# Two transformer blocks on one core: where the array's tiles begin, and value products with 128 columns

## The chip, the core and the metric

The kernel runs on one core of one Trainium2 chip. The core has a matrix engine (TensorE, PE in the profile; its weight loads are listed as PEld), a vector engine (VectorE, DVE), a scalar engine (ScalarE, ACT), GpSimd (POOL) and SyncE (SP), which issues most of the transfers. The metric is the device time of one execution in microseconds, the median over several runs.

## The reference

Two transformer blocks run one after the other on 512 tokens of width 1024, all in float32. The heart of it:

```python
# block 1
h = modulate(rmsnorm(x), ...);  proj = h @ w_in
s = q @ k.T * scale (+ rel_bias);  p = softmax(mask(s));  o = p @ v     # 8 MLA heads, 8 chunk-attention heads
x = x + g_a * (concat(o_mla, o_ca) @ w_out)
u = causal_dwconv(modulate(rmsnorm(x), ...) @ w_up);  x = x + g_m * ((silu(gate) * val) @ w_down)
# block 2
y_a = stick_breaking(q_a, k_a, v_a)          # 8 heads of 64: exp(log_sigmoid(z) + tail) @ v
y_b = retention(q_b, k_b, v_b)               # 8 heads of 64: (q k^T * decay) v, then group norm and gate
x = x + concat(y_a, y_b) @ w_out
x = x + moe(rmsnorm(x))                      # 32 experts, top 4, 1024 -> 2 x 1024 -> 1024
x = x + (p @ w_ple_proj) * sigmoid(rmsnorm(x) @ w_ple_gate)
```

A head is 64 wide in all three attentions' value products.

## The kernel before, in words

The stages follow one another: modulation and input projections to about 165 us, softmax attention to 285, output projection, the MLP's up projection from 400 to 570 and its down projection from 570 to 690, the projections of block 2, retention from 791 to 835, stick-breaking attention from 916 to 970, the experts from about 1060 to 2280, and the last gate.

**Dense products.** To keep float32 accuracy each large operand is split into a high and a low part in the array's one-pass format: `split` (L183) copies the value with ACT (L185) and subtracts with DVE (L188). A product is then three TensorE instructions (`mm3`): high by high, high by low, low by high. All of them go through `mm` (L165), so that the profile knows products by their tiles: `whi`/`wlo` and `hh`/`hl` are the parts of weights and of activations in block 1, `ah`/`al` the parts of the hidden activations, `mhi`/`mlo` the parts of the experts' weights `mraw`, `xh`/`xl` and `ah`/`al` the parts of an expert's 128 tokens. In the profile's rows the first name after the arrow is the moving operand, of 512 columns here, and the second the stationary one, of 128 columns. An f32 operand that is not split runs as one instruction that leaves two records.

**Attention.** The softmax attention goes through units (head, row block of 128 queries). At step s TensorE makes the scores of unit s, the transposes of unit s - 3 and the value product of unit s - 9. A value product (`pv`) has the head's 64 value columns as stationary operand and the transposed probabilities as moving one, with 512, 384, 256 or 128 columns. The two heads of a pair write the two halves, 64 partitions each, of one PSUM bank, and when the second head is done the bank is split into `hh` and `hl` at once. Retention (`rw` by `rv`) and stick-breaking (`sw` by `vs`) have the same layout, with 32 value products each; in the stick-breaking attention, whose products grow backwards over a bank, a product of a zero row first clears the pair's bank. PSUM has 8 banks of 128 x 512 that are handed out by `ps()`.

**Experts.** Weights come in chunks of 1 MB, issued by SP ahead of their use as buffers come free; ACT and DVE split each chunk; TensorE multiplies the split weights, as moving operand, by the tokens. The order on each engine is that of the program's text.

Of the kernel before, what the change touches and what calls it, by code (L numbers as in the profile page):

```python
# [10 lines left out]
F32 = mybir.dt.float32  # L11
F32R = mybir.dt.float32r
I32 = mybir.dt.int32
U32 = mybir.dt.uint32
AF = mybir.ActivationFunctionType
OP = mybir.AluOpType
# [6 lines left out]
NT = 4  # L23
P = 128
# [3 lines left out]
NE = 32  # L28
# [106 lines left out]
class Kernel:  # L135
# [343 lines left out]
    def softmax_attention(self, heads, pool, pool3, tail):  # L479
# [36 lines left out]
        def pv(hd, kt):  # L516
            par = hd["par"]
            if par == 0 and kt == 0:
                self.po = self.ps()
            rows = slice(64 * par, 64 * par + 64)  # L520
            self.mm(self.po[rows, kt * P:512], hd["v"](kt), hd["pT"][:, kt, kt * P:512], kt == 0, kt == NT - 1)
            if par == 1 and kt == NT - 1:
                return lambda po=self.po: self.split(po, self.hh[:, hd["pair"], :], self.hl_[:, hd["pair"], :])

# [40 lines left out]
    def block1(self, cg):  # L565
        nc, A = self.nc, self.A
        gp = self.pool("gp", 1, ctx=cg)
        self.ga = gp.tile([P, D], F32, name="ga")
        self.mcol = gp.tile([P, 48], F32, name="mcol")
        self.csil = gp.tile([P, 8], F32, name="csil")  # L570
# [167 lines left out]
        mp = self.pool("mla", 1, ctx=cm)  # L738
        gq = ap1.tile([P, 1], F32, name="gqs")
        nc.vector.tensor_scalar(gq, self.v("g_mq"), 96.0 ** -0.5, None, op0=OP.mult)  # L740
# [165 lines left out]
        for h in range(8):  # L906
            heads.append(dict(q=qTm[:, h, :], k=kTm[:, h, :], bias=None, par=h % 2, pair=h // 2,
                              v=lambda kt, h=h: vt[:, kt, h * 64:(h + 1) * 64]))
        for h in range(8):
            heads.append(dict(q=qTc[:, h // 2, :], k=kTc[:, h, :], bias=bias_for(h), par=h % 2,  # L910
                              pair=4 + h // 2, v=lambda kt, h=h: vc[:, kt, h * 64:(h + 1) * 64]))
        pso = []
# [122 lines left out]
    def block2_mix(self, right):  # L1035
        nc, A = self.nc, self.A
        cx = ExitStack()
        op = self.pool("o2", 1, ctx=cx)
        rx = op.tile([P, NT], F32, name="rx")
        self.row_rstd(self.ssx2, rx)  # L1040
# [38 lines left out]
        with ExitStack() as cr:  # L1079
# [48 lines left out]
            for s in range(len(units) + la):  # L1128
# [11 lines left out]
                if j >= 0:  # L1140
                    h, kt = units[j]
                    n = 512 - kt * P
                    rows = slice(64 * (h % 2), 64 * (h % 2) + 64)
                    if h % 2 == 0 and kt == 0:
                        po = self.ps()
                    self.mm(po[rows, kt * P:512], v[:, kt, h * 64:(h + 1) * 64], wt.pop(j)[:, 0:n], kt == 0,
                            kt == NT - 1)
                    if h % 2 and kt == NT - 1:
                        later = lambda h=h, po=po: nc.scalar.activation(yT[:, h // 2, :], po, AF.Copy)
            later()  # L1150
# [26 lines left out]
        self.zeros(qTs)  # L1177
        sc = os_.tile([P, 5, P], F32R, name="sc")
        idr, negr, trin, none, zero = [sc[:, i, :] for i in range(5)]
        for i, n in enumerate(("ident", "negm", "trin")):  # L1180
            nc.vector.tensor_copy(sc[:, i, :], self.cc(n))
        nc.vector.tensor_scalar(none, self.ones, -1.0, None, op0=OP.mult)
        nc.vector.tensor_scalar(zero, self.ones, 0.0, None, op0=OP.mult)
        cs = ExitStack()
# [35 lines left out]
        with ExitStack() as cs:  # L1220
# [7 lines left out]
            for s in range(len(units) + la3):  # L1228
# [35 lines left out]
                if 0 <= j < len(units):  # L1264
                    h, kt = units[j]
                    n = 512 - kt * P
                    rows = slice(64 * (h % 2), 64 * (h % 2) + 64)
                    if h % 2 == 0 and kt == 3:
                        po = self.ps()
                        self.mm(po, zero[0:1, :], sc[0:1, 0:4, :].rearrange("p a b -> p (a b)"), True, False)  # L1270
                    self.mm(po[rows, kt * P:512], vs[:, kt, h * 64:(h + 1) * 64], st.pop(j)[:, 0:n], False, kt == 0)
                    if h % 2 and kt == 0:
                        later[s + 2] = lambda h=h, po=po: self.split(po, self.hh[:, h // 2, :], self.hl_[:, h // 2, :])
        cx.close()
# [461 lines left out]
    def moe_open1(self, cx):  # L1736
# [6 lines left out]
        self.E4 = m1.tile([P, 2, NE], F32R, name="E4")  # L1743
        self.cnt = m1.tile([NE, 1], F32, name="cnt")
        for i in range(2):
# [24 lines left out]
    def moe_open3(self, cx):  # L1770
        self.mo = self.pool("mo", 1, ctx=cx, side="right")
        self.mo3 = self.pool("mo3", 6, ctx=cx, side="right")
        self.mx = self.pool("mx", 1, ctx=cx, side="right")
        m2 = self.pool("m2", 1, ctx=cx, side="right")
        self.xg = [m2.tile([P, D], F32, name="xg0")]
        self.g_n = 0
        self.nc.gpsimd.memset(self.xg[0], 0.0)
        self.ex = [self.expert(e) for e in range(NE)]
# [206 lines left out]
def build(nc, tc, A, out, dump=None):  # L1985
    with ExitStack() as ctx:
# [6 lines left out]
        K.ext = K.const.tile([1, 64], I32, name="ext")  # L1993
        K.extb = K.const.tile([P, 16], F32, name="extb")
        dr = K.pool("dr", 1, DRAM)
# [6 lines left out]
        with ExitStack() as right:  # L2002
            with ExitStack() as cr:
                big = K.pool("big", 1, ctx=cr)
                K.x = big.tile([P, NT, D], F32, name="x")
                K.ssx2 = big.tile([P, NT, 2], F32, name="ssx2")
                K.ssx3 = big.tile([P, NT, 2], F32, name="ssx3")
# [40 lines left out]
```

## Time and profile before

| what | value |
|---|---|
| median of 3 runs | 2365.99 us (2365.18 to 2371.5) |
| profiled execution | 2367.83 us |
| its span in the trace | 2365.7 us |
| TensorE busy | 2333.8 us, 99% of the span |
| VectorE busy | 1799.1 us, 76% |
| ScalarE busy | 1498.1 us, 63% |
| DMA traffic | 538.53 MB, mean 228 GB/s |

The profile is of one execution. Its own time is 1.8 us above the median, and its span is 2.1 us shorter than that time. A busy TensorE need not be at its peak: the time between the starts of two neighbouring products tells how fast it goes.

### The profile page before, as it was taken

The numbers are of one execution on the slowest core, as the hardware profiler recorded it, in microseconds if no ns is written. First come the engines' busy times: TensorE is split into PE (matmuls) and PEld (weight loads), VectorE is DVE, ScalarE is ACT, GpSimd is POOL, SyncE is SP. The second block draws the span as 40 slices with busy tenths as digits, with TensorE's granted clock in tenths as the row PEclk, the third lists the DMA queues.
The fourth block names the chain that finished last, engine by engine and source line by source line (L and its number), as shares of the span: only waits on it lengthen the run. The fifth ranks groups of instructions, "written<-read, shape, count | busy, mean of one in ns | idle before, by whom it ended". The sixth has DMA issues, their size and how long they took to land. (4 is left out here: it accounts for less than half of the span.)

```text
span 2365.7 us, 30628 instructions
## 1 busy us (share of the span) xinstructions
PE 2333.8 (99%) x10796; PEld 1849.6 (78%) x10796; DVE 1799.1 (76%) x2579; ACT 1498.1 (63%) x2201; POOL 165.1 (7%) x108
## 2 busy tenths in 40 slices
PE   9999999999999999989999999999999999999999
PEld 8874588888888576678888888888888888888877
DVE  6876676566557367559999999987799999999974
ACT  3676443334444237647778778775777778788764
POOL 0100000000000000010001101110010101101010
PEclk8999999999999999999999999999999999999999
DMA  9240333333233122259999999986999999999962
GB/s 326 88 131 13 123 115 125 115 108 108 98 109 99 43 89 72 96 185 337 334 356 342 356 351 342 361 295 218 330 361 356 347 358 335 362 346 342 332 198 107
DMA packets 282924, 538.53 MB, mean 228 GB/s; under 512 B 16277, under 2 KB 41397, under 8 KB 282576
## 3 DMA queue, kind: packets, MB, share of 16 engines
q1 hardware_dynamic: 268432, 508.08, 61.4%
q0 software_dynamic: 11792, 26.12, 4.1%
q10 hardware_dynamic: 2544, 2.34, 0.3%
q8 instruction: 86, 1.41, 0.2%
q14 instruction: 70, 0.57, 0.1%
HBM read 530.47 MB, written 23.59 MB: 234 GB/s over the span
## 5 line engine op out<-in xcount | busy, mean ns | idle before, releaser
L188 DVE TENSOR_TENSOR mlo<-mraw,mhi 128x1024 fp32r<-128x1024 f32 x777 | 911.3, 1219 | 118.7 <-ACT mhi L185 116.0
L185 ACT ACTIVATE mhi<-mraw 128x1024 fp32r<-128x1024 f32 x777 | 786.3, 1052 | 131.4 <-PE ps L165 110.4
L165 PE MATMUL ps<-mhi,xh 128*128 128x512 f32 x1024 | 409.6, 400 | 0.0
L165 PE MATMUL ps<-mhi,xl 128*128 128x512 f32 x1024 | 404.0, 395 | 0.2 <-DVE xl L1591 0.2
L165 PE MATMUL ps<-mlo,xh 128*128 128x512 f32 x1024 | 403.9, 394 | 0.0
L188 DVE TENSOR_TENSOR wlo<-raw,whi 128x1024 fp32r<-128x1024 f32 (+2 forms) x128 | 152.5, 1202 | 111.9 <-ACT whi L185 111.6
L165 PEld LDWEIGHTS ps<-mhi,xl 128*128 128x128 f32 x1024 | 192.7, 188 | 45.9 <-DVE xl L1591 0.6
L165 PEld LDWEIGHTS ps<-mlo,xh 128*128 128x128 f32 x1024 | 193.0, 188 | 42.4
L165 PEld LDWEIGHTS ps<-mhi,xh 128*128 128x128 f32 x1024 | 193.0, 188 | 41.3 <-ACT xh L1590 0.3
L185 ACT ACTIVATE whi<-raw 128x1024 fp32r<-128x1024 f32 (+2 forms) x128 | 132.5, 1042 | 135.0 <-PE ps L165 131.4
L165 PE MATMUL ps<-mhi,ah 128*128 128x512 f32 x512 | 203.1, 397 | 0.0
L165 PE MATMUL ps<-mhi,al 128*128 128x512 f32 x512 | 200.9, 392 | 0.0
L165 PE MATMUL ps<-mlo,ah 128*128 128x512 f32 x512 | 200.5, 392 | 0.0
L165 PE MATMUL ps<-whi,hh 128*128 128x512 f32 (+1 forms) x464 | 184.0, 397 | 5.1 <-ACT hh L185 2.3
L165 PE MATMUL ps<-wlo,hh 128*128 128x512 f32 (+1 forms) x464 | 180.8, 390 | 2.0 <-DVE wlo L188 2.0
L165 PE MATMUL ps<-whi,hl 128*128 128x512 f32 (+1 forms) x464 | 180.5, 389 | 0.0
L165 PE MATMUL ps<-hh,whi 128*128 128x512 f32 x352 | 137.8, 392 | 0.0
L165 PE MATMUL ps<-hh,wlo 128*128 128x512 f32 x352 | 136.9, 389 | 0.0
L165 PE MATMUL ps<-hl,whi 128*128 128x512 f32 x352 | 136.9, 389 | 0.0
L1644 ACT ACTIVATE mg<-mg 128x512 f32<-128x512 f32 x66 | 41.7, 632 | 141.5 <-DVE mg L1643 141.5
L165 PEld LDWEIGHTS ps<-mhi,al 128*128 128x128 f32 x512 | 96.1, 188 | 21.3
L165 PEld LDWEIGHTS ps<-mlo,ah 128*128 128x128 f32 x512 | 96.3, 188 | 20.4
(488 smaller groups left out, 3721.9 us busy)
## 6 DMA issues: line engine op xcount, KB each, us to landing
mraw<-in_w_ug SPq DMA_DIRECT2D x256, 1024.0 KB, 7.1
mraw<-in_w_dn SPq DMA_DIRECT2D x128, 1024.0 KB, 7.7
raw<-in_w_up SPq DMA_DIRECT2D x44, 512.0 KB, 3.6
raw<-in_w_in SPq DMA_DIRECT2D x40, 512.0 KB, 3.8
wa<-in_w_ada SPq DMA_DIRECT2D x12, 1024.0 KB, 11.8
raw<-in_w_ada SPq DMA_DIRECT2D x24, 512.0 KB, 4.6
raw<-in_w_down SPq DMA_DIRECT2D x22, 512.0 KB, 3.6
raw<-in_w_out SPq DMA_DIRECT2D x16, 512.0 KB, 4.8
```

The lines of the kernel that those rows point to most:

```text
L165: self.nc.tensor.matmul(out, l, r, start=start, stop=stop, skip_group_check=True)
L185: self.nc.scalar.activation(hi, raw, AF.Copy)
L188: self.nc.vector.tensor_tensor(lo, raw, hi, op=OP.subtract)
L1644: nc.scalar.activation(g, g, AF.Silu, scale=1.702)
```

## The change

It has three parts.

1. *Value products.* In all three attentions a head's value product takes the 128 value columns of its pair as stationary operand, writes all 128 partitions of a bank of its own, and only the head's 64 partitions of it are evacuated. The other 64 hold the neighbour's values under this head's probabilities and are not read. In place of one evacuation for each pair there is one for each head: 16 splits instead of 8 in the softmax attention, 8 copies instead of 4 in the retention, 8 splits instead of 4 in the stick-breaking attention.
2. *Zero products.* The stick-breaking attention's 4 zero products and their tile are gone; the first value product of a head starts its bank.
3. *Padding.* Some small tiles get more columns, which are not used, and one pool of small tiles 8 buffers instead of 6. What this does is to move the tiles that are allocated behind them.

```diff
-            par = hd["par"]
-            if par == 0 and kt == 0:
+            if kt == 0:
                 self.po = self.ps()
-            rows = slice(64 * par, 64 * par + 64)
-            self.mm(self.po[rows, kt * P:512], hd["v"](kt), hd["pT"][:, kt, kt * P:512], kt == 0, kt == NT - 1)
-            if par == 1 and kt == NT - 1:
-                return lambda po=self.po: self.split(po, self.hh[:, hd["pair"], :], self.hl_[:, hd["pair"], :])
+            self.mm(self.po[:, kt * P:512], hd["v"](kt), hd["pT"][:, kt, kt * P:512], kt == 0, kt == NT - 1)
+            if kt == NT - 1:
+                r = slice(64 * hd["par"], 64 * hd["par"] + 64)
+                return lambda po=self.po: self.split(po[r], self.hh[r, hd["pair"], :], self.hl_[r, hd["pair"], :])
...
-        self.mcol = gp.tile([P, 48], F32, name="mcol")
+        self.mcol = gp.tile([P, 96], F32, name="mcol")[:, 0:48]
...
-        gq = ap1.tile([P, 1], F32, name="gqs")
+        gq = ap1.tile([P, 56], F32, name="gqs")[:, 0:1]
...
-                              v=lambda kt, h=h: vt[:, kt, h * 64:(h + 1) * 64]))
+                              v=lambda kt, h=h: vt[:, kt, (h // 2) * P:(h // 2 + 1) * P]))
...
-        rx = op.tile([P, NT], F32, name="rx")
+        rx = op.tile([P, 56], F32, name="rx")[:, 0:NT]
...
-                    rows = slice(64 * (h % 2), 64 * (h % 2) + 64)
-                    if h % 2 == 0 and kt == 0:
+                    r = slice(64 * (h % 2), 64 * (h % 2) + 64)
+                    if kt == 0:
                         po = self.ps()
-                    self.mm(po[rows, kt * P:512], v[:, kt, h * 64:(h + 1) * 64], wt.pop(j)[:, 0:n], kt == 0,
+                    self.mm(po[:, kt * P:512], v[:, kt, (h // 2) * P:(h // 2 + 1) * P], wt.pop(j)[:, 0:n], kt == 0,
                             kt == NT - 1)
-                    if h % 2 and kt == NT - 1:
-                        later = lambda h=h, po=po: nc.scalar.activation(yT[:, h // 2, :], po, AF.Copy)
+                    if kt == NT - 1:
+                        later = lambda h=h, po=po, r=r: nc.scalar.activation(yT[r, h // 2, :], po[r], AF.Copy)
...
-                    if h % 2 == 0 and kt == 3:
+                    if kt == 3:
                         po = self.ps()
-                        self.mm(po, zero[0:1, :], sc[0:1, 0:4, :].rearrange("p a b -> p (a b)"), True, False)
-                    self.mm(po[rows, kt * P:512], vs[:, kt, h * 64:(h + 1) * 64], st.pop(j)[:, 0:n], False, kt == 0)
+                    self.mm(po[:, kt * P:512], vs[:, kt, (h // 2) * P:(h // 2 + 1) * P], st.pop(j)[:, 0:n], kt == 3,
+                            kt == 0)
...
-        self.cnt = m1.tile([NE, 1], F32, name="cnt")
+        self.cnt = m1.tile([NE, 33], F32, name="cnt")[:, 0:1]
...
-        self.mo3 = self.pool("mo3", 6, ctx=cx, side="right")
+        self.mo3 = self.pool("mo3", 8, ctx=cx, side="right")
...
-        K.extb = K.const.tile([P, 16], F32, name="extb")
+        K.extb = K.const.tile([P, 48], F32, name="extb")[:, 0:16]
...
-                K.ssx2 = big.tile([P, NT, 2], F32, name="ssx2")
+                K.ssx2 = big.tile([P, NT, 6], F32, name="ssx2")[:, :, 0:2]
```

Where the tiles that TensorE reads begin in a partition of SBUF, in bytes modulo 256, as the two programs place them:

| tiles | before | after |
|---|---|---|
| `hh`, `hl`, `whi`, `wlo` (block 1 and projections of block 2) | 64 | 0 |
| `ah`, `al` (hidden activations, MLP and experts) | 128 | 0 |
| `mhi`, `mlo`, `BD` (experts' weights, biases) | 192 | 64 |
| `xh`, `xl` (an expert's tokens) | 64 | 64 |
| `prob`, `pT`, `qTm`, `kTm`, `qTc`, `kTc` (softmax attention) | 192 | 0 |
| `qT`, `kT`, `rv`, `rw`, `qTs`, `kTs`, `vs`, `sw`, `sc`, `sh`, `sl` (retention, stick-breaking) | 128 | 0 |

Products with 512 moving columns of 2 KB begin their operands at the tile's start or a multiple of 256 bytes behind it, so the table holds for each of them.

How the change stands in the order of the engines' rows: on TensorE, in the softmax attention, three kinds of product take turns, the scores (`kTm`, `qTm`), the transposes of the probabilities (`cst`, `prob`, in groups of one to four) and the value products (`pT` by the values, whose tile is listed as `x`). Before:

```order
L165 MATMUL ps<-pT,x 64x512
L165 MATMUL ps<-kTm,qTm 128x384
L181 MATMUL ps<-cst,prob 128x128 x4
L165 MATMUL ps<-pT,x 64x384
L165 MATMUL ps<-kTm,qTm 128x512
L181 MATMUL ps<-cst,prob 128x128
```

And now:

```order
L165 MATMUL ps<-pT,x 128x512
L165 MATMUL ps<-kTm,qTm 128x384
L181 MATMUL ps<-cst,prob 128x128 x4
L165 MATMUL ps<-pT,x 128x384
L165 MATMUL ps<-kTm,qTm 128x512
L181 MATMUL ps<-cst,prob 128x128
```

The order is the same; the value products' rows have 128 output partitions where they had 64. So a width of 64 no longer stands between two of 128. Over the whole program, 248 pairs of neighbouring TensorE products have one stationary operand of 64 columns and one of 128 before, and 14 have now.

On TensorE in the stick-breaking attention (`sh` and `sl` with their numbers are the high and low part of one block's logarithms, `sc` the constants), at the start of a pair, before:

```order
L165 MATMUL ps<-sl_7619,sc 128x256
L165 MATMUL ps<-sh_7641,sc 128x384
L165 MATMUL ps<-sl_7642,sc 128x384
L165 MATMUL ps<-sc 128x512
L165 MATMUL ps<-sw,vs 64x128
L165 MATMUL ps<-qTs,kTs 128x384
```

And now:

```order
L165 MATMUL ps<-sl_7652,sc 128x256
L165 MATMUL ps<-sh_7674,sc 128x384
L165 MATMUL ps<-sl_7675,sc 128x384
L165 MATMUL ps<-sw,vs 128x128
L165 MATMUL ps<-qTs,kTs 128x384
```

The product of the zero row, `sc` into a whole bank, has gone from between the sums and the first value product.

On ACT in the softmax attention (L496 is the exponential, L555 or L556 the copy of the transposed probabilities, L185 the high part of a split), at the end of a head and of a pair, before:

```order
L556 ACTIVATE pT<-ps 128x2x128
L496 ACTIVATE prob,smx<-ps,nm 128x256
L556 ACTIVATE pT<-ps 128x3x128
L496 ACTIVATE prob,smx<-ps,nm 128x384
L556 ACTIVATE pT<-ps 128x4x128
L496 ACTIVATE prob,smx<-ps,nm 128x512
L556 ACTIVATE pT<-ps 128x128
L496 ACTIVATE prob,smx<-ps,nm 128x128
L556 ACTIVATE pT<-ps 128x2x128
L496 ACTIVATE prob,smx<-ps,nm 128x256
L185 ACTIVATE hh<-ps 128x512
L556 ACTIVATE pT<-ps 128x3x128
```

And now:

```order
L555 ACTIVATE pT<-ps 128x2x128
L496 ACTIVATE prob,smx<-ps,nm 128x256
L185 ACTIVATE hh<-ps 64x512
L555 ACTIVATE pT<-ps 128x3x128
L496 ACTIVATE prob,smx<-ps,nm 128x384
L555 ACTIVATE pT<-ps 128x4x128
L496 ACTIVATE prob,smx<-ps,nm 128x512
L555 ACTIVATE pT<-ps 128x128
L496 ACTIVATE prob,smx<-ps,nm 128x128
L555 ACTIVATE pT<-ps 128x2x128
L496 ACTIVATE prob,smx<-ps,nm 128x256
L185 ACTIVATE hh<-ps 64x512
```

The one split of 128 partitions, at the end of a pair, has become two of 64 partitions, one at the end of each head; DVE's low part (L188) follows each in the same way. ACT has 1278 rows before and 1289 now, DVE 1849 and 1858; SP and POOL have the same rows in the same order.

## Rows read from the trace of the kernel before

**Rows 1.** Page, parts 1 and 2: busy time, and the granted clock in 40 slices.
```profile
PE 2333.8 (99%) x10796; PEld 1849.6 (78%) x10796; DVE 1799.1 (76%) x2579; ACT 1498.1 (63%) x2201; POOL 165.1 (7%) x108
...
PEclk8999999999999999999999999999999999999999
```

**Rows 2.** The longest of TensorE's waits: total us, times, longest us.
```profile
PE ps L165 <- DVE cm L1364: 3.9, 1, 3.9
```

**Rows 3.** Page, part 5: groups of products (moving tile first, then stationary).
```profile
L165 PE MATMUL ps<-mlo,xh 128*128 128x512 f32 x1024 | 403.9, 394 | 0.0
...
L165 PE MATMUL ps<-mlo,ah 128*128 128x512 f32 x512 | 200.5, 392 | 0.0
...
L165 PE MATMUL ps<-wlo,hh 128*128 128x512 f32 (+1 forms) x464 | 180.8, 390 | 2.0 <-DVE wlo L188 2.0
...
L165 PE MATMUL ps<-hh,wlo 128*128 128x512 f32 x352 | 136.9, 389 | 0.0
```

**Rows 4.** Groups of TensorE products by form: the MLP's down projection.
```profile
L165 PE MATMUL ps<-wlo,ah 128*128 128x512 f32 x176 | 69.5, 395 | 0.0
```

**Rows 5.** Timeline of TensorE in the MLP's up projection: first and last of 27 starts.
```profile
449.82 0.39 PE L165 MATMUL ps<-hh,wlo 128*128 128x512 f32 x1
...
455.71 0.39 PE L165 MATMUL ps<-hl,whi 128*128 128x512 f32 x1
```

**Rows 6.** Timeline in the MLP's down projection: first and last of 26 starts.
```profile
600.00 0.40 PE L165 MATMUL ps<-whi,ah 128*128 128x512 f32 x1
...
605.83 0.39 PE L165 MATMUL ps<-wlo,ah 128*128 128x512 f32 x1
```

**Rows 7.** Timeline in the experts' products: 24 starts up, then 18 starts down.
```profile
1882.19 0.39 PE L165 MATMUL ps<-mhi,xh 128*128 128x512 f32 x1
...
1887.54 0.40 PE L165 MATMUL ps<-mhi,xl 128*128 128x512 f32 x1
...
1888.00 0.39 PE L165 MATMUL ps<-mhi,ah 128*128 128x512 f32 x1
...
1891.89 0.39 PE L165 MATMUL ps<-mhi,al 128*128 128x512 f32 x1
```

**Rows 8.** Timeline of TensorE and its weight loads (PEld) in the experts' products.
```profile
1200.40 0.40 PE L165 MATMUL ps<-mlo,ah 128*128 128x512 f32 x1
1200.40 0.19 PEld L165 LDWEIGHTS ps<-mhi,al 128*128 128x128 f32 x1
```

**Rows 9.** Timeline of TensorE in the retention (x2 is one f32 product).
```profile
811.25 0.86 PE L165 MATMUL ps<-rw,rv 128*64 128x384 f32 x2
812.04 0.91 PE L165 MATMUL ps<-qT,kT 128*128 128x384 f32 x2
812.88 0.65 PE L165 MATMUL ps<-rw,rv 128*64 128x256 f32 x2
```

**Rows 10.** Timeline of TensorE in the softmax attention.
```profile
210.02 0.91 PE L165 MATMUL ps<-kTm,qTm 128*128 128x384 f32 x2
210.77 0.60 PE L181 MATMUL ps<-cst,prob 128*128 128x128 f32 x4
```

**Rows 11.** Timeline of TensorE in the stick-breaking attention.
```profile
953.04 0.49 PE L165 MATMUL ps<-sc 1*128 1x512 f32 x1
953.46 0.43 PE L165 MATMUL ps<-sw,vs 128*64 128x128 f32 x2
```

**Rows 12.** Busy time by engine, softmax attention: PE, PEld, DVE, ACT, POOL, clock.
```profile
230.00:250.00 20.00, 20.00 (x78) 9.48 (x78) 13.04 (x65) 12.63 (x38) 1.61 (x3) 1.00 0.13 33
```

**Rows 13.** Waits in the softmax attention, 165 to 290 us.
```profile
DVE hl L188 <- ACT hh L185: 11.4, 8, 4.0
```

**Rows 14.** Busy time by engine in one head pair of the stick-breaking attention.
```profile
952.00:970.00 18.00, 18.00 (x83) 10.60 (x81) 10.61 (x26) 13.91 (x33) 0.00 (x0) 1.00 0.01 1
```

**Rows 15.** Busy time by engine in the experts' stage; last the DMA share.
```profile
1700.00:1800.00 100.00, 100.00 (x469) 82.19 (x468) 92.07 (x102) 77.75 (x96) 11.22 (x6) 1.00 1.03 365
```

**Rows 16.** Waits of SP's DMA queue in the experts' stage: total, times, longest.
```profile
SPq L1553 <- DVE mlo L188: 955.2, 361, 11.3
```

More of the change, by code (lines that the diff above doesn't have):

```diff
@@ L907, in block1 @@
             heads.append(dict(q=qTm[:, h, :], k=kTm[:, h, :], bias=None, par=h % 2, pair=h // 2,
-                              v=lambda kt, h=h: vt[:, kt, h * 64:(h + 1) * 64]))
+                              v=lambda kt, h=h: vt[:, kt, (h // 2) * P:(h // 2 + 1) * P]))
         for h in range(8):
             heads.append(dict(q=qTc[:, h // 2, :], k=kTc[:, h, :], bias=bias_for(h), par=h % 2,
-                              pair=4 + h // 2, v=lambda kt, h=h: vc[:, kt, h * 64:(h + 1) * 64]))
+                              pair=4 + h // 2, v=lambda kt, h=h: vc[:, kt, (h // 2) * P:(h // 2 + 1) * P]))
         pso = []
@@ L1177, in block2_mix @@
         self.zeros(qTs)
-        sc = os_.tile([P, 5, P], F32R, name="sc")
-        idr, negr, trin, none, zero = [sc[:, i, :] for i in range(5)]
+        sc = os_.tile([P, 4, P], F32R, name="sc")
+        idr, negr, trin, none = [sc[:, i, :] for i in range(4)]
         for i, n in enumerate(("ident", "negm", "trin")):
@@ L1182, in block2_mix @@
         nc.vector.tensor_scalar(none, self.ones, -1.0, None, op0=OP.mult)
-        nc.vector.tensor_scalar(zero, self.ones, 0.0, None, op0=OP.mult)
         cs = ExitStack()
@@ L1266, in block2_mix @@
                     n = 512 - kt * P
-                    rows = slice(64 * (h % 2), 64 * (h % 2) + 64)
-                    if h % 2 == 0 and kt == 3:
+                    r = slice(64 * (h % 2), 64 * (h % 2) + 64)
+                    if kt == 3:
                         po = self.ps()
-                        self.mm(po, zero[0:1, :], sc[0:1, 0:4, :].rearrange("p a b -> p (a b)"), True, False)
-                    self.mm(po[rows, kt * P:512], vs[:, kt, h * 64:(h + 1) * 64], st.pop(j)[:, 0:n], False, kt == 0)
-                    if h % 2 and kt == 0:
-                        later[s + 2] = lambda h=h, po=po: self.split(po, self.hh[:, h // 2, :], self.hl_[:, h // 2, :])
+                    self.mm(po[:, kt * P:512], vs[:, kt, (h // 2) * P:(h // 2 + 1) * P], st.pop(j)[:, 0:n], kt == 3,
+                            kt == 0)
+                    if kt == 0:
+                        later[s + 2] = lambda h=h, po=po, r=r: self.split(po[r], self.hh[r, h // 2, :],
+                                                                          self.hl_[r, h // 2, :])
         cx.close()
```

## The prediction

> **What bounds the kernel now.** I read the page's busy times first. TensorE is busy for 2333.8 of 2365.7 us and its clock was granted in full in all but the first slice [rows 1]; the longest single wait that its wait list shows is 3.9 us [rows 2]. So the time is a sum of TensorE's slots, a slot being the distance from the start of one product to the start of the next, and the change is worth what it does to those slots, as long as nothing else becomes late.
>
> Next come the groups of products [rows 3, 4] and the timelines [rows 5 to 7]. All of these are the same form, 128 stationary columns against 512 moving ones, yet they don't keep one pace. In the MLP's up projection 26 slots take 5.89 us, 226.5 ns each [rows 5]; in its down projection 25 take 5.83, 233.2 ns [rows 6]; in the experts' up products 23 take 5.35, 232.6 ns, and in their down products 17 take 3.89, 228.8 ns [rows 7]. The mean durations of the groups stand in the same order: 389 to 390 ns, 395, 394 and 392 [rows 3, 4] (a duration is longer than a slot because neighbours overlap). No row shows a wait in these stretches.
>
> What differs is in the table of tile starts. While one product streams its moving tile, the weight load of the next one reads that product's stationary tile: both start at 1200.40 [rows 8]. So the pair that meets is (start of the moving tile, start of the next stationary tile), modulo 256: (64, 64) for the MLP's up projection, (64, 128) for its down projection, (192, 64) for the experts' up products, (192, 128) for their down products. Taken as stationary less moving that is 0, 64, 128 and 192, with 226.5, 233.2, 232.6 and 228.8 ns. Equal starts go with the fastest slots. The heavy weight traffic of the experts' stage doesn't explain the order, because the slowest pair of all is in the MLP, which has less of it, and the experts' two kinds run in the same traffic 3.8 ns apart. My reading is that two reads of one memory disturb each other, depending on where in a 256-byte line they start; the traces of one kernel only show that the pace goes with the pair, not that it comes from it.
>
> **The alignment, costed.** The experts' up products come to 3 x 1024 = 3072 [rows 3] and go from (192, 64) to (64, 64). If they reach the MLP's pace, each saves 232.6 - 226.5 = 6.1 ns, together 18.7 us. If they only reach the pace of the experts' down products, it is 3.8 ns, 11.7 us. The groups' means give 394 - 389 = 5 ns. I take that: **15.4 us**. The MLP's down projection has 3 x 176 = 528 products [rows 4] and goes from (64, 128) to (0, 0): by the timelines 6.7 ns, by the means 395 - 389.5 = 5.5 ns, so 2.9 to 3.5 us; I take **3.2**. The experts' down products, 3 x 512 = 1536, go from (192, 128) to (64, 0); the difference stays at 192, so I take **0**, with a gain of 228.8 - 226.5 = 2.3 ns (3.5 us) and a loss of 232.6 - 228.8 = 3.8 ns (5.8 us) as its bounds. The MLP's up projection and what has its form, 3 x (464 + 352) = 2448 products, keeps equal starts, (64, 64) to (0, 0): nothing, as far as only the difference counts. Sum of the alignment: 18.6 us. The padding itself adds no instruction.
>
> **The value products, costed.** Two prices can be read. First, a change of the stationary width between 64 and 128 columns: the 384-column score product takes a slot of 0.84 us where a 64-column product follows (812.04 to 812.88) [rows 9], and 0.75 where a 128-column one does (210.02 to 210.77) [rows 10], so the change costs 0.09 us. The order of TensorE's rows has 248 such changes before and 14 after: 234 x 0.09 = 21.1 us saved. Second, an f32 product runs as two records, and the first one waits for its own weights: with 64 columns the 384-column product lasts 0.86 us, with 128 columns 0.91 [rows 9]. The wider load so costs 0.05 us in each of 128 value products, 6.4 us. The zero products: the slot from 953.04 to 953.46 is 0.42 us [rows 11], of which 0.09 is a change of width that is counted already; 4 x 0.33 = 1.3 us saved. Together 21.1 - 6.4 + 1.3 = 16.0 us.
>
> Against that stand the extra evacuations: one for each head in place of one for each pair, 8 more in the softmax attention and 4 more in each of the other two. They lie on ACT and DVE, which are busy 12.6 and 13.0 us of 20 in the softmax attention [rows 12] and 13.9 and 10.6 of 18 in the stick-breaking one [rows 14]; a pair's turn is about that long and gets one split more. That room is the cover. Without it each extra split can hold up the row maximum queued behind it on DVE, and with it the probabilities that TensorE transposes three steps on: DVE's wait for ACT's half was 11.4 us in 8 splits, 1.4 us each [rows 13]. The bounds are therefore 0 and 8 x 1.4 = 11.2 us. The products run three steps and more behind their inputs, so I am near the lower end and take off 1.3: **14.7 us**. The Trainium skill, page "TensorEngine Tiling (Array Packing)", section Overview, speaks against this half: a product with no more than 64 columns may gain up to 2x when it is placed as a tile beside another. The trace bears that out nowhere here, since the two heads' products of a pair stand a whole head apart and each is framed by full-width ones; by that rule the widening would lose time, by the rows it gains.
>
> Sum: 15.4 + 3.2 + 14.7 = 33.3 us. The profiled execution took 2367.8 us (2.1 of it outside the span), which gives 2334.5; it stood 1.8 above the median of 2366.0, so for the median I say **2333 us**.
>
> **Rivals.**
> 1. *The starts don't matter; pace and pair only go together by chance.* For it: with four pairs in four stages, each stage has its own tiles, traffic and order. Against it: the pace of a stage is nearly constant to the nanosecond, and the traffic gives the wrong order. Then only the value products count: 2366.0 - 14.7 = 2351, or 2348 if the MLP's down projection still answers. The Trainium skill, page "TensorE: Matmul & The Clock Gate", section "Step-by-step: what each phase is for", says this: the array has two independent read ports, so loading the next weights takes no bandwidth from the running product. By that rule the alignment is worth nothing; the four paces above are what speaks against it.
> 2. *The attention swallows its gain.* Extra splits, each with a wait of 1.4 us as above, and one more PSUM bank in use, make TensorE wait. For it: ACT at 13.9 of 18 us [rows 14]. With nothing left of the 14.7 the time is 2366.0 - 18.6 = 2347.
> 3. *Another engine takes over in the experts' stage.* DVE is busy 92.1 of 100 us there and the DMA share is 1.03 at 365 GB/s [rows 15]. A pace 5 / 232.6 = 2% higher on two thirds of the products needs some 93.4 of DVE. Against it: SP's queue waits 955 us for DVE to free buffers [rows 16], so the transfers run ahead. If the stage can't go faster, the 15.4 are lost: 2348.
> 4. *Slower: a tile start at 0 streams worse.* No row has a moving tile that starts at 0, and the 2448 + 528 + 1536 = 4512 products of the MLP's form and of the experts' down projection get a start at 0 in their pair. The other terms give 15.4 + 14.7 = 30.1 us, so from 30.1 / 4512 = 6.7 ns on the kernel is slower, and from 8.2 ns by more than 7 us. With 10 ns it is 2366.0 - 30.1 + 45.1 = 2381. Against it: the dearest known pair is 6.7 ns above the cheapest.
>
> **How the numbers follow.** Forecast 0.68, rival 1 0.14, rival 2 0.08, rival 3 0.05, rival 4 0.05. The forecast alone spans 2322 (18.7 + 3.5 + 3.5 + 16.0 and 1.5 for what isn't counted, 43.2 saved) to 2342 (11.7 + 2.9 + 14.7 - 5.8 = 23.5 saved). Up to 2350 lie rivals 2 and 3 and half of rival 1: range **2322 to 2350**. A change under 0.3%, about 7 us, can't be told from none. Faster by more: the forecast and rivals 1 to 3 (0.95), less 0.03 for rivals 1 and 2 together, 0.92. Within 0.3%: that 0.03 and 0.01 of rival 4, 0.04. Slower: 0.04.
>
> **What the profile after would show.** Right: slots near 227 ns in the experts' up products and in the MLP's down projection, 229 in the experts' down products, 226.5 in the MLP's up projection; a 384-column score slot of 0.75 us in the retention, a value product of 384 columns at 0.91; TensorE's waits no longer than now, DVE at 93 to 94 of 100 in the experts' stage. Wrong: experts' up slots that stay at 232 (rival 1); gaps on TensorE with ACT or DVE as the releaser in the attention stages (rival 2); gaps with mlo or a DMA as releaser among the experts (rival 3); the MLP's up projection above 230 ns (rival 4).

## The result, and the profile after

The changed kernel takes 2326.61 us in the median of 4 runs (2324.31 to 2331.82), the kernel before 2368.04 us in 4 runs beside it. The ratio is 0.9828 with a 95% interval of 0.9805 to 0.985: 41.4 us less, where 33 were forecast. The profiled execution is the longest of the four, 2331.82 us, so differences between the two traces come out some 5 us smaller than those between the medians. Timed again later, beside the experiments below, the changed kernel took 2330.65 us against 2369.09, 38.4 us less: the gain is some 38 to 41 us.

The page of the profile of the changed kernel, its span, busy times, clock, and the groups that answer to [rows 3]:

```profile
span 2329.7 us, 30633 instructions
...
PE 2285.1 (98%) x10792; PEld 1865.8 (80%) x10792; DVE 1805.1 (77%) x2590; ACT 1504.9 (65%) x2217; POOL 164.7 (7%) x108
...
PEclk8999999999999999999999999999999999999999
...
L165 PE MATMUL ps<-mlo,xh 128*128 128x512 f32 x1024 | 399.3, 390 | 0.0
...
L165 PE MATMUL ps<-mlo,ah 128*128 128x512 f32 x512 | 199.4, 389 | 0.0
...
L165 PE MATMUL ps<-wlo,hh 128*128 128x512 f32 (+1 forms) x464 | 181.1, 390 | 2.9 <-DVE wlo L188 2.9
...
L165 PE MATMUL ps<-hh,wlo 128*128 128x512 f32 x352 | 137.0, 389 | 0.0
```

The groups by form, for the MLP's down projection, as in [rows 4]:

```profile
L165 PE MATMUL ps<-wlo,ah 128*128 128x512 f32 x176 | 68.5, 389 | 0.0
```

TensorE's busy time fell by 48.7 us, its span by 36. The MLP's down product went from 395 to 389 ns, the experts' up product from 394 to 390, the MLP's up products stayed at 389 to 390. The same on the timeline of TensorE, the first and the last start of four stretches (MLP up, MLP down, experts' down, experts' up), as in [rows 5 to 7]:

```profile
439.75 0.39 PE L165 MATMUL ps<-hh,whi 128*128 128x512 f32 x1
...
451.99 0.39 PE L165 MATMUL ps<-hh,whi 128*128 128x512 f32 x1
...
589.78 0.39 PE L165 MATMUL ps<-wlo,ah 128*128 128x512 f32 x1
...
601.79 0.39 PE L165 MATMUL ps<-whi,ah 128*128 128x512 f32 x1
...
1851.43 0.39 PE L165 MATMUL ps<-mhi,ah 128*128 128x512 f32 x1
...
1856.69 0.39 PE L165 MATMUL ps<-mhi,al 128*128 128x512 f32 x1
...
1857.59 0.39 PE L165 MATMUL ps<-mhi,xh 128*128 128x512 f32 x1
...
1862.83 0.39 PE L165 MATMUL ps<-mhi,xl 128*128 128x512 f32 x1
```

A slot is again the distance from one start to the next. The MLP's up projection has 54 slots in 12.24 us, 226.7 ns each. Its down projection has 53 in 12.01, 226.6 ns: it was 233.2. The experts' down products have 23 in 5.26, 228.7 ns: as before. Their up products have 23 in 5.24, 227.8 ns: they were 232.6. So far this is the forecast.

In the attention it isn't. The timeline of the retention, to set beside [rows 9]:

```profile
796.44 0.81 PE L165 MATMUL ps<-rw,rv 128*128 128x384 f32 x2
797.09 0.81 PE L165 MATMUL ps<-qT,kT 128*128 128x384 f32 x2
797.73 0.59 PE L165 MATMUL ps<-rw,rv 128*128 128x256 f32 x2
```

The 384-column score product has a slot of 0.64 us (797.09 to 797.73); it was 0.84, and 0.75 was expected. The value product has 0.65 and was 0.79; 0.75 was expected (0.79 less the switch, plus the load). Its two records together last 0.81 us, not 0.91: with 128 columns it is shorter than it was with 64.

By stage, from the first to the last score or value product of each attention and from the first to the last product of the others (starts in the two traces; us):

| stage | before | after | difference |
|---|---|---|---|
| softmax attention | 116.4 | 108.5 | -7.9 |
| MLP's down projection | 124.7 | 121.4 | -3.3 |
| retention | 44.1 | 34.4 | -9.7 |
| stick-breaking attention | 73.1 | 63.7 | -9.4 |
| experts | 1235.8 | 1223.7 | -12.2 |
| sum | | | -42.5 |

The stick-breaking attention runs from 909.8 to 982.9 us in the kernel before, longer than the stretch named ahead of the prediction. The sum is 6.5 us more than the 36 us of the spans, and two places account for the difference: TensorE's longest wait, for `cm` between the attentions and the experts, was 6.2 us in this execution where [rows 2] has 3.9 (in the next profile of the same kernel it was 3.9 again), and the end of the experts' stage, told of below, lost 4.8.

The softmax attention gained least though it has half of the value products. The wait list of TensorE there (total us, times, longest):

```profile
engine line waited for: us in total, times, longest us
PE ps L181 <- DVE ps L493: 6.6, 10, 1.6
PE ps L181 <- DVE prob L514: 1.5, 5, 0.7
```

### The profile page after: what moved, and what is told of

Read it like the earlier page. It is cut to its first block, busy times and chain, and to the rows that moved or that the text cites. A ratio compares the mean times of both kernels' runs of the same rounds, so it can differ in the third digit from the quotient of the medians.

```text
span 2329.7 us, 30633 instructions
## 1 busy us (share of the span) xinstructions
PE 2285.1 (98%) x10792; PEld 1865.8 (80%) x10792; DVE 1805.1 (77%) x2590; ACT 1504.9 (65%) x2217; POOL 164.7 (7%) x108
## 5 line engine op out<-in xcount | busy, mean ns | idle before, releaser
L188 DVE TENSOR_TENSOR mlo<-mraw,mhi 128x1024 fp32r<-128x1024 f32 x777 | 909.3, 1219 | 108.7 <-ACT mhi L185 104.9
L185 ACT ACTIVATE mhi<-mraw 128x1024 fp32r<-128x1024 f32 x777 | 784.3, 1052 | 117.3 <-PE ps L165 108.0
L188 DVE TENSOR_TENSOR wlo<-raw,whi 128x1024 fp32r<-128x1024 f32 (+2 forms) x128 | 153.3, 1207 | 110.7 <-ACT whi L185 110.4
L185 ACT ACTIVATE whi<-raw 128x1024 fp32r<-128x1024 f32 (+2 forms) x128 | 132.6, 1043 | 130.7 <-PE ps L165 128.7
```

Of the source, the lines that this page charges most:

```text
L185: self.nc.scalar.activation(hi, raw, AF.Copy)
L188: self.nc.vector.tensor_tensor(lo, raw, hi, op=OP.subtract)
```

## The experiments

Each kernel was timed in rounds beside the kernel before; differences are between the medians of the two. Slots are means over all neighbouring pairs of such products of a run's trace that start less than 300 ns apart, about 2800 up and 1400 down in the experts' stage.

**The padding alone.** The kernel before with the seven padding lines of the diff and nothing else, for example:

```diff
-        self.cnt = m1.tile([NE, 1], F32, name="cnt")
+        self.cnt = m1.tile([NE, 33], F32, name="cnt")[:, 0:1]
...
-        self.mcol = gp.tile([P, 48], F32, name="mcol")
+        self.mcol = gp.tile([P, 96], F32, name="mcol")[:, 0:48]
```

> The kernel before with the padding alone: tiles start where they do in the changed kernel, the attention's value products keep 64 columns. Theory (the pace of a 512-column product goes with the next stationary tile's start less the moving tile's, modulo 256, and with nothing else of the change): the experts' up slots fall from 232.4 to about 228.6 ns (3072 products, 12 us) and the MLP's down slots from 233.3 to 227.1 (528 products, 3.3 us), the attention stages keep their length: about 15 us less than before. Rival (the attention's gain came from its tiles' new starts as well): some 13 us more, 28 less than before. Rival (the starts do nothing): 0.

Measured: 2352.39 us against 2367.67, 15.3 less, ratio 0.9939 (0.9925 to 0.9952). Experts' up slots 228.4 ns, MLP's down slots 227.1, down slots of the experts 229.1; retention 44.07 us and stick-breaking 73.11 us long, as before, softmax attention 117.4 where it was 116.4. The starts are worth their whole gain without the rest, and give the attention nothing.

**The value products alone.** The changed kernel with the padding taken out again.

> The changed kernel without its padding: value products with 128 columns and a bank per head, no zero products, all tiles that the array reads at the starts of before. Theory (every change of the stationary width costs the switch and also uncovers the weight load of the product after it, so about 0.34 us for each value product): retention 9.9 us shorter, stick-breaking 9 us, softmax attention 8 us, together 27 us, experts and MLP unchanged: about 27 less than before. Rival (the prediction's own model: an f32 product pays its load always, only the switch goes): 15 less. Rival (half of the attention's gain is due to tile starts): 14 less.

Measured: 2341.65 us against 2367.67, 26.0 less, ratio 0.9894 (0.9879 to 0.9909). Retention 34.42 us, stick-breaking 63.72, softmax attention 109.4, where the changed kernel has 34.42, 63.71 and 108.5; the experts' slots are those of before (232.4 and 229.3 ns). Retention and stick-breaking are as short as in the changed kernel, so the tiles' starts have no share in their gain, and the prediction's model of it, good for 15 us, falls. The two parts add up, 15.3 + 26.0 = 41.3 against 41.4; that they agree to 0.1 us is chance, since each has an interval of 3 us and more on either side.

**The retention by twos.** The kernel before; only the retention's order differs:

```diff
-            la = 3
+            la = 2
...
-            for s in range(len(units) + la):
-                if s < len(units):
+            for s0 in range(0, len(units) + la, 2):
+                for s in (s0, s0 + 1):
+                    if s < len(units):
...
-                j = s - la
...
+                for j in (s0 - la, s0 - la + 1):
```

> The kernel before with the retention's products in another order: two score products, then two value products, which keep 64 columns. 64 changes of width become 32. Theory (a change costs the switch, 0.09 us, and uncovers the load of the product after it, 0.05 for 64 columns and 0.10 for 128): 16 pairs x 0.34 = 5.4 us less in the retention. Rival (the load of an f32 product is never covered): 32 x 0.09 = 3.0 us less. Rival (a product of 64 columns is slow by itself, whatever stands beside it): 0.

Measured: 2365.16 us against 2367.67, ratio 0.9988 (0.9979 to 0.9997), which is 2.5 us less, between 0.7 and 5.0. Taken by itself that is nearer to the rival's 3.0 than to 5.4, and the run times don't decide. The trace does: the retention is 39.29 us long where it was 44.07, 4.8 less. The expectation had counted 64 changes falling to 32; in the traces there are 57, as the last products of the stage stand together, and they fall to 29. With 28 fewer the theory gives 14 x 0.34 = 4.8, the rival 28 x 0.09 = 2.5. Its timeline on TensorE (x4 are two f32 products of two records):

```profile
808.31 1.72 PE L165 MATMUL ps<-rw,rv 128*64 128x512 f32 x4
809.96 1.77 PE L165 MATMUL ps<-qT,kT 128*128 128x512 f32 x4
811.66 0.86 PE L165 MATMUL ps<-rw,rv 128*64 128x256 f32 x4
812.46 0.92 PE L165 MATMUL ps<-qT,kT 128*128 128x256 f32 x4
```

Two value products with 512 and 384 moving columns take 1.65 us here (808.31 to 809.96); apart they took 1.00 (the slots of its two records 480 and 522 ns) and 0.79 [rows 9]. Record by record, each by its slot: the first record of the product behind a change of width keeps its 480 ns (512 moving columns, 64 stationary ones), that of the product behind one of the same width falls from 373 to 322 (384 columns); the last record ahead of a change keeps its 416 (384 columns), that ahead of none falls from 522 to 429 (512 columns). The same holds for the scores: 533 stays (512 columns), 427 falls to 322 (384 columns). So a 64-column product isn't slow by itself, and its load is covered as soon as its neighbour has its width. (Each 64-column product here also takes a tile of 128 x 64 of the array, `128*64` in its rows; no run tells the number of columns from the tile.)

**Another pair for the experts' up products.** The changed kernel, with two unused tiles more:

```diff
+        self.pool("pad1", 1, ctx=cx, side="right").tile([P, 16], F32, name="pad1")
         self.mhl = self.pool("mhl", 6, ctx=cx, side="right")
...
+        self.pool("pad2", 1, ctx=cx, side="right").tile([P, 48], F32, name="pad2")
         self.mx = self.pool("mx", 1, ctx=cx, side="right")
```

> The changed kernel with two more unused tiles, which put the experts' weights at 0, tokens still at 64, hidden activations at 0. Pairs: up (0, 64), difference 64; down (0, 0), difference 0. Theory (the difference sets the pace): up slots rise from 228.6 to about 233 ns, as the MLP's down projection had with difference 64, and down slots fall from 229.1 to 227 to 228.6: 3072 x 4.6 - 1536 x 1 = 12 us more than the changed kernel, that is some 29 less than before. Rival (an absolute start of 192 was slow, any of 0 and 64 is fast): as the changed kernel, 41 less than before.

Measured: 2336.92 us against 2367.67, 30.8 less, ratio 0.987 (0.9855 to 0.9885): 8 to 10 us worse than the changed kernel by its two measurements, and 12.3 us by the length of the experts' stage in the trace (1235.9 against 1223.7). The experts' timeline on TensorE, first and last start of 23 up slots and of 23 down slots:

```profile
1851.73 0.39 PE L165 MATMUL ps<-mhi,xh 128*128 128x512 f32 x1
...
1857.09 0.39 PE L165 MATMUL ps<-mhi,xl 128*128 128x512 f32 x1
...
1857.56 0.39 PE L165 MATMUL ps<-mhi,ah 128*128 128x512 f32 x1
...
1862.77 0.39 PE L165 MATMUL ps<-mhi,al 128*128 128x512 f32 x1
```

Up slots 233.0 ns, down slots 226.5 (over the whole stage 233.1 and 228.5). None of these tiles begins at 192 any more, and the up products are as slow as they were. Both kinds now have a moving tile at 0 and are 4.6 ns apart, so the moving tile's own start doesn't set the pace either.

**The same differences at other starts.** The changed kernel with unused tiles that put the experts' weights and tokens at 128 and the hidden activations at 64 (48 columns ahead of `mhl`, 16 ahead of `ml`).

> The changed kernel with two more unused tiles, which put the experts' weights and tokens at 128 and the hidden activations at 64: pairs (128, 128) and (128, 64) in place of (64, 64) and (64, 0), the same differences, 0 and 192, at other starts. Theory (only the difference counts): slots of 228.3 and 229.1 ns as in the changed kernel, no change of time. Rival (starts at 0 or 64 are what is fast, one at 128 is slow): up slots at 232 ns or more, 11 us more than the changed kernel.

Measured: 2333.41 us against 2369.09, ratio 0.985 (0.9835 to 0.9865); the changed kernel itself, run beside it, 2330.65, ratio 0.9837 (0.9824 to 0.985). The timeline, 23 down slots and 23 up slots:

```profile
1853.70 0.40 PE L165 MATMUL ps<-mhi,ah 128*128 128x512 f32 x1
...
1859.07 0.40 PE L165 MATMUL ps<-mhi,al 128*128 128x512 f32 x1
...
1859.97 0.40 PE L165 MATMUL ps<-mhi,xh 128*128 128x512 f32 x1
...
1865.22 0.39 PE L165 MATMUL ps<-mhi,xl 128*128 128x512 f32 x1
```

The up slots, pair (128, 128), are 228.3 ns here and 229.0 over the stage, 0.6 more than (64, 64) has. The down slots, pair (128, 64), are 233.5 here and 231.2 over the stage, not 229.1. The expectation held for the one pair to within 1 ns and failed for the other by 2 ns, which is 3 us of 1536 products. That starts at 128 are slow, the rival, is out: it needed up slots of 232 ns or more.

**Difference 192 once more.** The changed kernel with weights at 0, tokens and hidden activations at 192 (16, 16 and 48 columns of padding).

> The changed kernel with three more unused tiles: the experts' weights at 0, tokens and hidden activations at 192, so that up and down pairs are both (0, 192), difference 192. Theory (the difference sets the pace): up and down slots both at 229.1 ns, as (64, 0) had; up loses 3072 x 0.8 = 2.5 us, 2 to 3 us more than the changed kernel. Rival (each pair has a pace of its own, as (128, 64) with 231 suggests): anything between 227 and 233, so up to 14 us more.

Measured: 2331.13 us against 2368.31, ratio 0.9842 (0.9829 to 0.9856). The timeline, 23 down slots and 23 up slots:

```profile
1853.63 0.39 PE L165 MATMUL ps<-mhi,ah 128*128 128x512 f32 x1
...
1858.89 0.39 PE L165 MATMUL ps<-mhi,al 128*128 128x512 f32 x1
...
1859.79 0.39 PE L165 MATMUL ps<-mhi,xh 128*128 128x512 f32 x1
...
1865.06 0.39 PE L165 MATMUL ps<-mhi,xl 128*128 128x512 f32 x1
```

228.7 and 229.1 ns, over the stage 229.5 and 229.6, both kinds of product alike, as the theory has it, and 0.4 to 0.5 ns above its 229.1.

**Low part later.** The changed kernel; in the softmax attention DVE makes the low part of a split one step after ACT has made the high part:

```diff
-                return lambda po=self.po: self.split(po[r], self.hh[r, hd["pair"], :], self.hl_[r, hd["pair"], :])
+                hi, lo = self.hh[r, hd["pair"], :], self.hl_[r, hd["pair"], :]
+                return (lambda po=self.po: nc.scalar.activation(hi, po[r], AF.Copy),
+                        lambda po=self.po: nc.vector.tensor_tensor(lo, po[r], hi, op=OP.subtract))
...
+            if low:
+                low()
+                low = None
             if later:
-                later()
+                later[0]()
+                low = later[1]
                 later = None
```

> The changed kernel, with the low part of each split in the softmax attention made one step later than its high part, so that DVE no longer stands waiting for ACT with the row maxima queued behind it. Theory (TensorE's waits of 8.7 us in that stage come from the 16 splits): most of them go, 5 to 8 us less than the changed kernel. Rival (the stage is now bound by the way from scores to probabilities, three steps ahead, splits or not): 0 to 1 us less.

Measured: 2321.76 us against 2369.09, ratio 0.98 (0.9786 to 0.9813), 8.9 less than the changed kernel run beside it. TensorE's waits in the softmax attention:

```profile
engine line waited for: us in total, times, longest us
PE ps L181 <- DVE ps L493: 3.1, 3, 1.6
PE ps L181 <- DVE prob L514: 0.6, 1, 0.6
```

The stage is 100.0 us long, 8.4 less.

**The same on the kernel before.** The same edit on the kernel before, with whole pairs.

> The kernel before, with the low part of the softmax attention's splits made one step later than the high part, as in the earlier run on the changed kernel. Theory (before the change TensorE was the slower side of that stage, and DVE's wait of 11.4 us lay in its shadow): 0 to 0.5 us less than before. Rival (the splits had held TensorE up before as well, and the later low part is worth some 8 us in any case): 8 us less.

Measured: 2367.67 us against 2368.31, ratio 0.9999 (0.999 to 1.0008). Nothing, as expected: TensorE's wait for the row maxima in that stage is 3.5 us in 4 times with the edit and without it.

**The hidden activations at 64.** The changed kernel with 16 unused columns ahead of `ml`, and beside these runs the changed kernel itself.

> The changed kernel with one more unused tile, which puts the experts' hidden activations at 64, as the weights: the down pair goes from (64, 0) to (64, 64). Theory (equal starts are the best that a pair can be, and in the experts' stage they measured 228.4 against 229.1 ns): 1536 x 0.7 = 1 us less than the changed kernel, within what can't be told from none. Rival (equal starts give the MLP's 227.1 ns): 3 us less.

> The changed kernel itself, again, beside the following three on the same chip: 0.9828 of the time before, some 41 us less.

Measured: 2327.7 us, ratio 0.9831 (0.9818 to 0.9845), against 2330.65 for the changed kernel, 0.9837 (0.9824 to 0.985). The intervals overlap, so the run times don't show a gain. The trace has down slots of 228.2 ns in place of 229.1, which is 1.4 us.

**Both edits.**

> The changed kernel with the later low part in the softmax attention and with the experts' hidden activations at 64. Theory (the two gains, 8.9 and 1.5 to 3 us as measured each by itself, lie in different stages and add up): 50 us less than before, a ratio of 0.979.

Measured: 2318.48 us against 2368.31, 49.8 less, ratio 0.9792 (0.9779 to 0.9806). It is the fastest of the kernels here.

## Why the prediction was right, and what in it was not

**The bound.** Right. TensorE's slots made the time, and both parts acted through them. One reading was too coarse: a 9 in [rows 1] is 90% or more, and the clock wasn't granted in full behind the first slice throughout (0.94 from 170 to 190 us and 0.96 from 1000 to 1050 in the kernel before). In the experts' stage no other engine took over, which was rival 3; the windows by engine and the queue's waits, to set beside [rows 15, 16]:

```profile
1900.00:2000.00 100.00, 100.00 (x473) 82.42 (x472) 94.20 (x119) 80.02 (x102) 13.72 (x10) 1.00 1.01 345
```

```profile
SPq L1552 <- DVE mlo L188: 943.0, 361, 10.6
```

DVE is busy 94.2 of 100 us (92.1 from 1700 to 1800, the stretch of [rows 15]), TensorE all of the time, and SP's queue still waits 943 us for buffers.

**The alignment.** Mechanism right, size a little large. The up products were to fall by 5 ns, 15.4 us, and fell by 232.4 - 228.4 = 4.0, 12.3 us, inside the bounds of 11.7 and 18.7. The MLP's down projection was to give 3.2 and gave 3.3. The experts' down products (0) and the MLP's up projection (0) gave 0.3 and 0. That is 15.9 by slots, and 15.3 measured by the padding alone, where 18.6 was forecast. The mis-sized term is the 5 ns: it came from setting the experts' 394 ns against the MLP's 389, and with equal starts the experts' slots come down to 228.4 ns only, not to the MLP's 226.7; no run tells why. Rival 1 (the starts do nothing) is contradicted: the same instructions in the same order are 6 ns apart in the MLP's down projection by their tiles' starts alone. The page of the Trainium skill beside it, "TensorE: Matmul & The Clock Gate", section "Step-by-step: what each phase is for", by which loading the next weights takes no bandwidth from the running product, doesn't agree with that either: with the moving tile at 0, the next stationary tile at 64 costs 233.1 ns and at 0 228.5. Rival 4, that a start at 0 streams worse, is contradicted by (0, 0) with 227.1 ns.

That the difference of the starts sets the pace held for these pairs (moving, next stationary), slots in ns over a stage:

| difference | pairs and slots |
|---|---|
| 0 | MLP (64, 64) 226.7, (0, 0) 226.7 (up) and 227.1 (down); experts (64, 64) 228.2 to 228.4, (0, 0) 228.5, (128, 128) 229.0 |
| 64 | MLP (64, 128) 233.3; experts (0, 64) 233.1 |
| 128 | experts (192, 64) 232.4 |
| 192 | experts (192, 128) 229.3, (64, 0) 229.1, (0, 192) 229.6, (128, 64) 231.2 |

The last pair is out of line by some 2 ns, and one pair can hold two paces: in the changed kernel, pair (64, 0), slots from `mhi` by `ah` to `mlo` by `ah` take 230.7 ns and those from `mlo` by `ah` to `mhi` by `al` 227.2, with the same starts modulo 256. No run tells why. A period longer than 256 bytes isn't needed: as the programs place the tiles, the differences of (192, 128) and (64, 0) are 448 and 192 modulo 512, with 229.3 and 229.1 ns. So the difference is what orders the pairs to within 2 ns, not the whole rule. Why 64 and 128 cost 4 to 6 ns is open too: that two reads disturb each other, as the prediction has it, fits these rows, but no run looks at the reads themselves.

**The value products.** Here a step failed, though the range held the result. It reads: "Second, an f32 product runs as two records, and the first one waits for its own weights: with 64 columns the 384-column product lasts 0.86 us, with 128 columns 0.91 [rows 9]. The wider load so costs 0.05 us in each of 128 value products, 6.4 us." The durations were read rightly, but all of those products stood behind a change of width. The load is uncovered only there, as the weight loads (PEld) of the 384-column score product show, in the kernel before and in the changed one:

```profile
812.04 0.30 PEld L165 LDWEIGHTS ps<-qT,kT 128*128 128x128 f32 x2 [0.60 <-issue]
```

```profile
796.77 0.51 PEld L165 LDWEIGHTS ps<-qT,kT 128*128 128x128 f32 x2
```

Behind a 64-column product the first load starts with its own product, at 812.04 [rows 9]; behind one of 128 columns it starts at 796.77, 0.32 us ahead of its product at 797.09, while the product before it still runs. In place of a loss of 0.05 us the load term is a gain of 0.05 for the value product and of 0.10 for the product behind it; with two switches of 0.09 that is 0.34 us (0.05 + 0.10 + 0.19) for each value product that stood between wider ones. The Trainium skill, page "TensorE: Matmul & The Clock Gate", section "LDWEIGHTS (loading the stationary operand)", lets a load's time go with its columns alone, at columns / 1.2 in ns, by which 64 and 128 columns are an estimate of 53 and 107; what is uncovered here, 480 - 429 = 51 and 533 - 429 = 104 ns, agrees. The retention shows it in full: 29 changes into a value product at 0.093 + 0.051 us and 28 out of one at 0.093 + 0.104 make 9.7 us, and 9.7 went. The order by twos shows that the width of the neighbours is the cause and not the number of columns or the starts.

**The evacuations.** Also mis-sized, the other way. The forecast took off 1.3 us for them, between bounds of 0 and 11.2. In the softmax attention, with the slots of the two traces set side by side, those without a wait became 17.2 us shorter, and those that hold a wait in either trace 9.2 longer, so that 7.9 are left. How one wait comes about is on the timeline of three engines in the changed kernel:

```profile
203.58 0.59 ACT L185 ACTIVATE hh<-ps 64x512 fp32r<-64x512 f32 x1
...
204.20 0.69 DVE L188 TENSOR_TENSOR hl<-ps,hh 64x512 fp32r<-64x512 f32 x1 [1.12 <-ACT hh L185]
...
204.91 0.11 DVE L493 MEMSET ps<- 64x64 f32 x1
...
205.72 0.34 DVE L514 TENSOR_SCALAR prob<-prob,rc 128x256 f32<-128x256 f32 x1
206.07 0.11 DVE L493 MEMSET ps<- 64x64 f32 x1
...
206.21 0.41 PE L181 MATMUL ps<-cst,prob 128*128 128x128 f32 x2 [0.44 <-DVE ps L493]
```

ACT makes the high part of a head's split; DVE, in order, has been idle for 1.12 us when it can subtract, and only then starts on the scores' mask and maximum behind it, and on the probabilities (L514) that the next transposes read. Those are done at 206.06, the next mask follows at 206.07, and TensorE resumes at 206.21 after an idle 0.44. (The profile names the mask as what ended the wait; by the program the transposes need L514.) The busy times by engine in the same 20 us as [rows 12]:

```profile
230.00:250.00 20.00, 19.48 (x92) 12.39 (x91) 16.06 (x78) 14.72 (x43) 2.15 (x4) 1.00 0.15 41
```

TensorE is busy 19.48 of 20 us where it was 20.00, DVE 16.06 where it was 13.04. The cover named, a lookahead of three steps, was there while TensorE's own steps were the slower side; made faster by 15%, the steps are no longer long enough for DVE's idle microsecond. The room was also tighter than the prediction had it: a pair's turn is 13 us in this stage (104 us for 8 pairs), not about 20. The later low part gives 8.4 us back, and the same edit on the kernel before nothing, so the cover was real and the change used it up. Whether the eight further splits or the faster pace used it up is not shown: that edit moves all 16 splits. Rival 2 came true for about half of that stage's gain, and the forecast's sign that TensorE's waits would be no longer than before failed here.

The two errors have opposite signs: 36.3 us (17.2 + 9.7 + 9.4) were to be had in the attention where 16.0 were forecast, and 9.2 were lost to waits where 1.3 were. The value products alone measured 26.0, not 14.7; with 15.3 for the starts, not 18.6, that is why 33 became 41. That the time still fell inside the range is in part luck: the waits and the smaller gain of the starts took back half of what the load term had wrong. With that error alone some 54 us would have gone, more than the range allowed.

**Open.** At the end of the experts' stage the first products of the last gate start after an idle time that grew. In the changed kernel and in the kernel before:

```profile
2268.90 3.36 PE L165 MATMUL ps<-mraw 128*128 128x512 f32 x7 [5.70 <-ACT mhi L185]
```

```profile
2306.36 5.73 PE L165 MATMUL ps<-mraw 128*128 128x512 f32 x24 [2.31 <-issue]
```

5.70 us against 2.31. During that wait the granted clock fell; the window of the 6.8 us that it lasted has, behind the engines' busy times, a clock of 0.50:

```profile
2266.00:2272.80 6.80, 3.90 (x9) 3.13 (x10) 4.63 (x4) 4.14 (x5) 0.00 (x0) 0.50 0.99 341
```

That is the lower of the clock's two levels, 1.2 GHz in place of 2.4. The kernel before has no such stretch there. From the last down product to the end of the span it is 74.2 us in the changed kernel and 69.4 in the one before, so this place costs 4.8 us, 3.4 of them the longer wait. Both profiles of the changed kernel and those of three of its variants have the long wait, with 5.3 to 5.7 us; three other variants, and the kernels with one part alone, stay at 2.3 to 2.4. The padding alone, with a wait of 2.3, still has 3.4 us at the lower clock, so the long wait isn't its only condition. The releaser named is not always the same (ACT's `mhi` here, DVE's `mlo` in the next profile of the same kernel), and no run was made for it.

## What to carry to other kernels

When TensorE is the bound, list the distances between starts of products of one form, stage by stage: a form that has two paces is hiding something, here where two tiles begin modulo 256 bytes, and the cure costs a few unused columns (equal starts were the best pair, or within 1 ns of it, wherever they were tried). An f32 product whose stationary operand is narrower than its neighbours' is dear through them: it costs the switch on both sides and uncovers two weight loads, so price it by the slots of its neighbours too, and don't read a cost as the product's own when every instance stands in the same surroundings. When TensorE gets faster in a stage, look at what waits in order on the other engines there: an ACT-then-DVE pair on one step is a wait that the old pace hid.

## What the runs showed that was not expected

The weight load of an f32 product with 128 stationary columns is covered entirely behind a product of the same width: the first record of a 512-column score product has a slot of 429 ns there, as the second does, and 533 behind a 64-column product. Among products of 128 stationary columns, one more of that width so takes less than one of 64 (its two records last 0.81 us for 384 moving columns, against 0.86). And the pair (128, 64) at 231.2 ns, with the same difference as three pairs at 229 to 230.
